# Differential attention pairs: values as the stationary operand in two column tiles, mean square by a product with a block matrix

## The chip, the cores and the metric

The kernel runs on one core of a Trainium2 chip. The metric is the device time of one execution in microseconds. The program is one launch; the host only lays the arrays out.

## The reference, cut to what matters

One layer of a decoder trunk over 256 positions of 1024 features: a SwiGLU mixer, a token mixer of three attention branches, and a second SwiGLU mixer, each followed by a layer norm. The token mixer projects x to queries, keys and values of the three branches and to gates, and merges the branches' outputs by sigmoid gates. Six heads of 64 per branch. The change touches the differential branch alone:

```python
def diff_attention(q, k, v, slopes, lam, subln_g, lambda_init):
    ...
        s = jnp.einsum('bhmcd,bhmsd->bhmcs', qc, k).astype(F32) * scale
        s = jnp.where(dist >= 0, s - slope * dist, -jnp.inf)
        p = jax.nn.softmax(s, axis=-1)
        w = p[:, :, 0] - lam * p[:, :, 1]
        return jnp.einsum('bhcs,bhsd->bhcd', w.astype(v.dtype), v)
    ...
    o = o * lax.rsqrt(jnp.mean(jnp.square(o), axis=-1, keepdims=True) + SUBLN_EPS) * subln_g
    return (o * (1.0 - lambda_init)).astype(v.dtype)
```

So each head has two softmax maps, their weighted difference multiplies the values, and each position's 64 outputs are divided by their root mean square.

## The kernel before

All large products run on TensorE in float32r, with each operand split into a rounded part and a rest: `Weights.split` (L104 to L111) makes both parts of a weight chunk of 128 x 1024, ScalarE the rounded one and VectorE the rest, from a raw buffer that a DMA filled. Nine split buffers and five raw ones go round; `done` gives a buffer back when its products are through, and `pump` splits and loads the next.

The token mixer works through the table `MIX`: projections of queries and keys for one pair of heads (`project`), gate products (`gates`) and branch outputs (`branch`). A pair of heads is a list of stages, and `slot` runs one stage of each pair under way, in the order of the kinds in `KINDS`; so a slot holds, say, the last stage of one pair, the transposes of the next and the scores of a third. The class `Pe` counts TensorE's time as the program is written and starts a slot, at least `PACE` = 10 us after the one before, in the middle of a projection or of gate products. That count only sets the order in which the instructions are written: each engine then works through its own queue in that order and waits for semaphores. For the last 2.2 us before a slot (`QUIET`) no weight split is written.

PSUM has eight banks, four named `acc` and four named `att`. The `att` banks go round: the fifth request takes the first bank again, and the first product in it waits until the bank's last reader is through.

A differential pair has two heads with two maps each, so four score banks (two of each name) and four weight tiles `e` of 128 x 384 (the lower triangle of 256 x 256 in two pieces). Its stages before: `start` makes the scores, the exponentials with their row sums `sm`, and `combine`s e0 + c e1 on VectorE, with c = -lambda sum0/sum1; `turn` transposes the two combined tiles on TensorE and ScalarE copies them to SBUF as `eT`; `pv` multiplies with the transposed weights as the stationary operand (six products with 64 columns), scales the rows by 1/sum0, and computes the mean square on VectorE with the power -1/2 on GpSimd; `scale`, due 2.5 us later, multiplies by it; `turn_o` transposes the output (two transposes), and `act_split` copies it to `oT` and its rest. The other two kinds of pair, `moba_pair` and `stick_pair`, already use `values_T`: the values are the stationary operand, 64 columns for each head of the pair in two column tiles, so that the output comes out transposed.

Of the kernel before, what the change touches and what calls it, by code (L numbers as in the profile page):

```python
# [53 lines left out]
T_M = 3.4  # L54
N_T = 4.5
M_N = 2.0
D_S = 2.5
E_BUFS = 6


class Weights:
# [129 lines left out]
def trunk(ctx: ExitStack, tc: tile.TileContext, start_d, x_d, ln_g, ln_b, gu_d, gun_d, down_d, v_d, qk_d, gate_d,  # L191
# [364 lines left out]
    with ExitStack() as es:  # L556
# [76 lines left out]
        def values_T(b, p, eTs):  # L633

            po = att.tile([P, 512], F32, name="att")
            for kt, cs, ws in ((0, slice(0, S), slice(0, S)), (1, slice(P, S), slice(S, BW))):
                for r in range(2):
                    pe.mm(po[r * HD:(r + 1) * HD, cs], V[:, kt, vcol(b, 2 * p + r)], eTs[r][:, ws], kt == 0, kt == 1,
                          tile_position=(0, r * 64), share=2, skip_group_check=True)
            act_split(oT[b][:, p, 0:S], oT[b][:, p, S:2 * S], po[:, 0:S])  # L640
            pairs_done[b] += 1

# [3 lines left out]

        KINDS = ("sums", "turn_o", "pv", "turn", "valT", "scores")

        def moba_pair(p, qT, kT):
            sm = small.tile([P, 2, 2], F32, name="sm")
# [23 lines left out]
        def diff_pair(p, qT, kT):  # L676
# [4 lines left out]
            def start():  # L681
                banks = [(acc if i < 2 else att).tile([P, 512], F32, name="acc" if i < 2 else "att")
                         for i in range(4)]
                scores([(i * 32, 32, banks[i]) for i in range(4)], qT, kT, True)
                ee.extend(ep.tile([P, BW], F32, name="e") for _ in range(4))
                exp_rows([(banks[i], SLOPES[2 * (2 * p + i // 2) + 1], ee[i], nmx[:, i % 2, i // 2, :],
                           sm[:, i % 2, i // 2, :]) for i in range(4)])
                exps[0] -= 1

                def combine(r):  # L690
                    c = small.tile([P, 2], F32, name="c")
                    nc.vector.reciprocal(c, sm[:, 1, r, :])
                    nc.vector.scalar_tensor_tensor(c, sm[:, 0, r, :], nlam, c, op0=ALU.mult, op1=ALU.mult)
                    e0, e1 = ee[2 * r], ee[2 * r + 1]
                    for t, cs in enumerate((slice(0, P), slice(P, BW))):
                        nc.vector.scalar_tensor_tensor(e0[:, cs], e1[:, cs], c[:, t:t + 1], e0[:, cs],
                                                       op0=ALU.mult, op1=ALU.add)
                for r in range(2):
                    combine(r)

            def pv():
                ps = att.tile([P, 512], F32, name="att")
                for r in range(2):
                    vc, eT = vcol(1, 2 * p + r), eTs[r]
                    o0, o1 = ps[:, r * HD:(r + 1) * HD], ps[:, P + r * HD:P + (r + 1) * HD]
                    pe.mm(o0, eT[:, 0:P], V[:, 0, vc], True, True)
                    pe.mm(o1, eT[:, P:S], V[:, 0, vc], True, False)
                    pe.mm(o1, eT[:, S:BW], V[:, 1, vc], False, True)
                rs = small.tile([P, 2, 2], F32, name="rsm")
                nc.vector.reciprocal(rs, sm[:, 0])  # L710
                o = ep.tile([P, S], F32, name="o", bufs=1)
                o4 = o.rearrange("p (t r c) -> p t r c", t=2, r=2)
                nc.vector.tensor_tensor(
                    o4, ps[:, 0:S].rearrange("p (t r c) -> p t r c", t=2, r=2),
                    rs.rearrange("p r t -> p t r").unsqueeze(3).to_broadcast([P, 2, 2, HD]), op=ALU.mult)
                sq = ep.tile([P, S], F32, name="s1", bufs=3)
                nc.vector.tensor_tensor(sq, o, o, op=ALU.mult)
                ms = small.tile([P, 4], F32, name="ms")
                nc.vector.tensor_reduce(ms, sq.rearrange("p (a c) -> p a c", c=HD), axis=mybir.AxisListType.X,
                                        op=ALU.add)  # L720
                nc.vector.tensor_scalar(ms, ms, 1.0 / HD, EPS, op0=ALU.mult, op1=ALU.add)
                nc.gpsimd.tensor_tensor(ms, ms, mhalf[:, 0:4], op=ALU.pow)
                os_.append(o)

                def scale():
                    nc.vector.tensor_tensor(
                        o4, o4, ms.rearrange("p (t r) -> p t r", t=2).unsqueeze(3).to_broadcast([P, 2, 2, HD]),
                        op=ALU.mult)
                pe.later(D_S, scale)

            def turn_o():
                ps = att.tile([P, 512], F32, name="att")
                for t in range(2):
                    pe.tr(ps[:, t * P:(t + 1) * P], os_[0][:, t * P:(t + 1) * P], ident)
                act_split(oT[1][:, p, 0:S], oT[1][:, p, S:2 * S], ps[:, 0:S])
                pairs_done[1] += 1

            return [{"scores": start},
                    {"turn": lambda: eTs.extend(turn_rows(e) for e in ee[::2])},
                    {"pv": pv},  # L740
                    {"turn_o": turn_o}]

        def stick_pair(p, qT, kT):
            zs, wts, split = [], [], []
# [229 lines left out]
```

## Time and profile before

| what | us |
|---|---|
| median of 3 runs | 598.71 (598.22 to 599.05) |
| the profiled execution | 598.51 |
| its span, first to last instruction | 596.8 |
| TensorE busy | 587.8 (98%) |
| VectorE busy | 407.5 (68%) |
| ScalarE busy | 328.2 (55%) |
| GpSimd busy | 32.4 (5%) |

The profile is of one execution; 1.7 us of its time lie outside the span. PE is TensorE's products, PEld its weight loads (which run beside products), DVE is VectorE, ACT ScalarE, POOL GpSimd, SP the queue that issues the loads. A product's end is modelled, so pieces of the chain, which are cut by start and release, are better prices than its busy time.

### The profile page before, as it was taken

What the parts mean: (1) busy time and instruction counts of PE and PEld (TensorE: products, weight loads), DVE (VectorE), ACT (ScalarE), POOL (GpSimd) and SP (SyncE); (2) the same over time, 40 slices, a digit from 0 to 9 for tenths busy, and PEclk for the clock granted to TensorE, in tenths of its full rate; (3) what the DMA queues carried; (4) which work ended last, traced back from release to release, by engine and by line L of the source; (5) the groups of instructions that cost most, each with busy time, mean ns of one, the idle gap of its engine ahead of it and who ended that gap; (6) DMA issues with size and microseconds to landing.
All of it is one profiled execution on the core that took longest, in us unless ns stands there. A gap on an engine that the chain in (4) does not pass through costs nothing.

```text
span 596.8 us, 8546 instructions
## 1 busy us (share of the span) xinstructions
PE 587.8 (98%) x3150; PEld 505.2 (85%) x3150; DVE 407.5 (68%) x655; ACT 328.2 (55%) x556; POOL 32.4 (5%) x71
## 2 busy tenths in 40 slices
PE   8999999999999999999999999999999999999995
PEld 7888888888888998888888878888898898888884
DVE  6889767674338746597977685889867667774217
ACT  5868656663312758596657654535665655654100
POOL 1610000000001002110001000001000000000001
PEclk9999999999999999999999999999999999999998
DMA  8999755666431576354547447256965565565001
GB/s 320 316 392 314 241 187 180 207 188 226 141 125 63 200 258 237 118 176 150 171 139 245 145 158 264 97 183 217 330 229 177 180 202 186 180 207 178 1 0 70
DMA packets 32538, 113.34 MB, mean 190 GB/s; under 512 B 3681, under 2 KB 4449, under 8 KB 32497
## 3 DMA queue, kind: packets, MB, share of 16 engines
q1 hardware_dynamic: 30672, 106.77, 53.2%
q0 software_dynamic: 1680, 5.83, 3.0%
q8 instruction: 24, 0.39, 0.3%
q10 hardware_dynamic: 144, 0.20, 0.1%
q14 instruction: 18, 0.14, 0.1%
HBM read 111.74 MB, written 1.05 MB: 189 GB/s over the span
## 4 chain that ended last, share of the span: by engine, by line
PE 97%; DMA 1%; DVE 1%; issue 0%; SPq 0%; ACT 0%; DVEq 0%
PE acc L182 91%; PE att L182 4%; PE att L186 2%; DMA sraw<-start 1%; DVE x L364 0%; DVE x L360 0%; ACT w L275 0%; DVE st L448 0%; DVE x L447 0%; SPq L249 0%; DVEq L968 0%; SPq L246 0%; DVE mv L353 0%
## 5 line engine op out<-in xcount | busy, mean ns | idle before, releaser
L107 DVE TENSOR_TENSOR w<-raw,w 128x1024 fp32r<-128x1024 f32 (+1 forms) x166 | 197.8, 1208 | 61.7 <-ACT w L106 60.8
L182 PE MATMUL acc<-xT,w 128*128 128x512 f32 (+1 forms) x1264 | 226.4, 337 | 0.0
L182 PEld LDWEIGHTS acc<-xT,w 128*128 128x128 f32 x1264 | 196.3, 190 | 26.6 <-issue 1.0
L106 ACT ACTIVATE w<-raw 128x1024 fp32r<-128x1024 f32 (+1 forms) x166 | 170.3, 1042 | 52.2 <-PE acc L182 44.0
L182 PE MATMUL acc<-w,xT 128*128 128x512 f32 (+1 forms) x576 | 128.1, 379 | 0.0
L182 PEld LDWEIGHTS acc<-w,xT 128*128 128x128 f32 x576 | 105.5, 188 | 18.6 <-issue 1.0
L182 PE MATMUL acc<-w,hT 128*128 128x512 f32 (+1 forms) x408 | 93.1, 383 | 0.0
L182 PEld LDWEIGHTS acc<-w,hT 128*128 128x128 f32 x408 | 75.2, 188 | 14.9
L475 ACT ACTIVATE lo<-acc 128x256 f32<-128x256 f32 x76 | 28.8, 384 | 57.3 <-PE acc L182 57.3
L477 DVE TENSOR_TENSOR gu<-acc,lo 128x256 f32<-128x256 f32 x76 | 31.6, 423 | 34.7 <-ACT lo L475 34.6
L182 PE MATMUL acc<-xT,wx 128*128 128x256 f32 (+1 forms) x240 | 46.1, 337 | 0.0
L107 DVE TENSOR_TENSOR wx<-raw,wx 128x1024 fp32r<-128x1024 f32 (+1 forms) x30 | 36.3, 1214 | 12.5 <-ACT wx L106 12.5
L182 PEld LDWEIGHTS acc<-xT,wx 128*128 128x128 f32 x240 | 37.5, 190 | 4.4
L106 ACT ACTIVATE wx<-raw 128x1024 fp32r<-128x1024 f32 (+1 forms) x30 | 31.3, 1047 | 11.3 <-PE acc L182 10.2
L354 ACT ACTIVATE rs<-mv 128x1 f32<-128x1 f32 x6 | 1.2, 204 | 59.6 <-DVE mv L353 59.6
L182 PE MATMUL acc<-wx,hT 128*128 128x512 f32 (+1 forms) x138 | 32.8, 380 | 0.0
L182 PEld LDWEIGHTS acc<-wx,hT 128*128 128x128 f32 x138 | 25.2, 188 | 4.9
L355 POOL TENSOR_TENSOR rs<-rs,mhalf 128x1 f32<-128x1 f32 x6 | 5.3, 892 | 407.9 <-ACT rs L354 407.9
L346 DVE SCALAR_TENSOR_TENSOR x<-x,acc 128x512 f32<-128x512 f32 x11 | 7.5, 683 | 27.4 <-PE acc L182 27.4
L182 PE MATMUL acc<-w,oT 128*128 128x512 f32 x108 | 25.7, 393 | 0.0
L182 PEld LDWEIGHTS acc<-w,oT 128*128 128x128 f32 x108 | 20.1, 188 | 4.4 <-issue 0.3
L236 ACT ACTIVATE hT<-gu 128x256 fp32r<-128x256 f32 x38 | 15.8, 417 | 11.5 <-DVE gu L482 11.5
(146 smaller groups left out, 412.9 us busy)
## 6 DMA issues: line engine op xcount, KB each, us to landing
raw<-gu SPq DMA_DIRECT2D x76, 512.0 KB, 4.8
raw<-down SPq DMA_DIRECT2D x44, 512.0 KB, 4.2
raw<-gates SPq DMA_DIRECT2D x24, 512.0 KB, 4.4
raw<-qk SPq DMA_DIRECT2D x18, 512.0 KB, 4.5
raw<-v SPq DMA_DIRECT2D x12, 384.0 KB, 3.0
raw<-w_out SPq DMA_DIRECT2D x8, 512.0 KB, 4.3
raw<-gun SPq DMA_DIRECT2D x8, 512.0 KB, 4.3
sraw<-start SPq DMA_DIRECT2D x7, 384.0 KB, 6.6
```

What stands on the lines that cost most here:

```text
L106: self.nc.scalar.activation(h[:, :n], raw[:, :n], AF.Copy)
L107: self.nc.vector.tensor_tensor(l[:, :n], raw[:, :n], hv[:, :n], op=ALU.subtract)
L182: self.nc.tensor.matmul(out, lhsT=lhsT, rhs=rhs, start=start, stop=stop, **kw)
L186: self.nc.tensor.transpose(out, in_, ident)
L236: nc.scalar.activation(dst_h, src, AF.Copy)
L346: nc.vector.scalar_tensor_tensor(xs, xs, ALPHA, ps[:, 0:n], op0=ALU.mult, op1=ALU.add)
L354: nc.scalar.activation(rs, mv[:, 1:2], AF.Copy, bias=EPS)
L355: nc.gpsimd.tensor_tensor(rs, rs, mhalf[:, 0:1], op=ALU.pow)
L475: nc.scalar.activation(lo, ps[:, S:2 * S], AF.Copy)
L477: nc.vector.tensor_tensor(v, ps[:, 0:S], lo, op=ALU.add)
```

## The change

Of the differential pair, from the exponentials on, everything but the transposes of the weights is rewritten. The rows are now normalised before the values: ScalarE scales the tiles of the first map by 1/sum0, VectorE adds the second map times -lambda/sum1. The values use `values_T`. The output is then transposed already, 64 features of each head on 64 partitions; its square is split into two float32r parts and multiplied by a 128 x 128 block matrix with entries 1/64, which gives each position's mean square on all 64 partitions. The power -1/2 is the exponential of -0.5 times the logarithm on ScalarE, followed by one Newton step on VectorE. `KINDS` and the number of `e` buffers change with it.

```diff
-D_S = 2.5
-E_BUFS = 6
+E_BUFS = 4
...
+            if b == 1:
+                return po
...
-        KINDS = ("sums", "turn_o", "pv", "turn", "valT", "scores")
+        KINDS = ("sums", "turn", "valT", "scores")
...
+        mean64 = ep.tile([P, P], F32R, name="mean64", bufs=1)
...
-                def combine(r):
-                    c = small.tile([P, 2], F32, name="c")
-                    nc.vector.reciprocal(c, sm[:, 1, r, :])
-                    nc.vector.scalar_tensor_tensor(c, sm[:, 0, r, :], nlam, c, op0=ALU.mult, op1=ALU.mult)
+                rs = small.tile([P, 2, 2, 2], F32, name="rsd")
+                nc.vector.reciprocal(rs, sm)
+                nc.vector.tensor_scalar(rs[:, 1], rs[:, 1], nlam, None, op0=ALU.mult)
+                for r in range(2):
                     e0, e1 = ee[2 * r], ee[2 * r + 1]
                     for t, cs in enumerate((slice(0, P), slice(P, BW))):
-                        nc.vector.scalar_tensor_tensor(e0[:, cs], e1[:, cs], c[:, t:t + 1], e0[:, cs],
+                        nc.scalar.activation(e0[:, cs], e0[:, cs], AF.Copy, scale=rs[:, 0, r, t:t + 1])
+                    for t, cs in enumerate((slice(0, P), slice(P, BW))):
+                        nc.vector.scalar_tensor_tensor(e0[:, cs], e1[:, cs], rs[:, 1, r, t:t + 1], e0[:, cs],
                                                        op0=ALU.mult, op1=ALU.add)
...
-            def pv():
+            def values():
+                po = values_T(1, p, eTs)
+                o = ep.tile([P, S], F32, name="o", bufs=1)
+                nc.scalar.activation(o, po[:, 0:S], AF.Copy)
+                sq = ep.tile([P, S], F32, name="s1", bufs=3)
+                nc.vector.tensor_tensor(sq, po[:, 0:S], o, op=ALU.mult)
+                sp = ep.tile([P, 2 * S], F32R, name="sq", bufs=1)
+                act_split(sp[:, 0:S], sp[:, S:2 * S], sq)
+                os_.extend((o, sp))
+
+            def rms():
+                o, sp = os_
                 ps = att.tile([P, 512], F32, name="att")
...
-            def turn_o():
-                ps = att.tile([P, 512], F32, name="att")
-                for t in range(2):
-                    pe.tr(ps[:, t * P:(t + 1) * P], os_[0][:, t * P:(t + 1) * P], ident)
-                act_split(oT[1][:, p, 0:S], oT[1][:, p, S:2 * S], ps[:, 0:S])
+                for n in range(2):
+                    pe.mm(ps[:, 0:S], mean64, sp[:, n * S:(n + 1) * S], n == 0, n == 1)
+                f = ep.tile([P, S], F32, name="s1", bufs=3)
+                nc.scalar.activation(f, ps[:, 0:S], AF.Ln, bias=eps_c)
+                nc.scalar.activation(f, f, AF.Exp, scale=-0.5)
+
+                c = ep.tile([P, S], F32, name="s1", bufs=3)
+                nc.vector.scalar_tensor_tensor(c, ps[:, 0:S], EPS, f, op0=ALU.add, op1=ALU.mult)
+                nc.vector.tensor_tensor(c, c, f, op=ALU.mult)
+                nc.vector.tensor_scalar(c, c, -0.5, 1.5, op0=ALU.mult, op1=ALU.add)
+                nc.vector.tensor_tensor(o, o, f, op=ALU.mult)
+                nc.vector.tensor_tensor(o, o, c, op=ALU.mult)
+                act_split(oT[1][:, p, 0:S], oT[1][:, p, S:2 * S], o)
                 pairs_done[1] += 1
...
                     {"turn": lambda: eTs.extend(turn_rows(e) for e in ee[::2])},
-                    {"pv": pv},
-                    {"turn_o": turn_o}]
+                    {"valT": values},
+                    {"sums": rms}]
```

The order on TensorE in the slot that holds the last stage of the first differential pair, before. The `att` numbers tell the requests apart; `e` are the tiles of the third differential pair, which are transposed, and `kT`, `qT` make the first MoBA pair's scores.

```order
L186 MATMUL att_3034<-ident_117,o_2864 128x128 x2
L182 MATMUL att_3039<-V_1892,eT_2876 128x64 x3
L182 MATMUL att_3039<-V_1892,eT_2882 128x64 x3
L186 MATMUL att_3056<-ident_117,e_2896 128x128 x3
L186 MATMUL att_3062<-ident_117,e_2898 128x128 x3
L182 MATMUL att_3068<-kT_3017,qT_3013 128x128
L182 MATMUL att_3069<-kT_3017,qT_3013 128x128
```

The same slot on TensorE after the change.

```order
L181 MATMUL att_3039<-sq_2886,mean64_2136 128x256 x2
L185 MATMUL att_3053<-ident_117,e_2901 128x128 x3
L185 MATMUL att_3059<-ident_117,e_2903 128x128 x3
L181 MATMUL att_3065<-eT_2869,V_1892 64x256
L181 MATMUL att_3065<-eT_2875,V_1892 64x256
L181 MATMUL att_3065<-eT_2869,V_1892 64x128
L181 MATMUL att_3065<-eT_2875,V_1892 64x128
L181 MATMUL att_3077<-kT_3022,qT_3018 128x128
L181 MATMUL att_3078<-kT_3022,qT_3018 128x128
```

Six banks are requested in the slot both times, from four; the two score banks are the slot's first and second request come round again. Before, these were the banks of the output's transposes and of the values; now they are those of the mean square (att_3039) and of the first transposed weights (att_3053).

ScalarE's queue from the projection's copies (`s1`) to the next weight split (`w`) in that slot, before.

```order
L826 ACTIVATE s1_3012<-acc_2978,qsc_215 128x256
L829 ACTIVATE s1_3016<-acc_2979 128x256
L236 ACTIVATE oT1_1894<-att_3034 128x256
L630 ACTIVATE eT_3060<-att_3056 128x384
L630 ACTIVATE eT_3066<-att_3062 128x384
L106 ACTIVATE w_3080<-raw_2829 128x1024
```

The same piece of ScalarE's queue after the change; L729 is the logarithm, L730 the exponential, L716 the values' copy.

```order
L829 ACTIVATE s1_3017<-acc_2983,qsc_215 128x256
L832 ACTIVATE s1_3021<-acc_2984 128x256
L729 ACTIVATE s1_3042<-att_3039,eps_c_2142 128x256
L730 ACTIVATE s1_3042<-s1_3042 128x256
L235 ACTIVATE oT1_1894<-o_2882 128x256
L629 ACTIVATE eT_3057<-att_3053 128x384
L629 ACTIVATE eT_3063<-att_3059 128x384
L716 ACTIVATE o_3070<-att_3065 128x256
L235 ACTIVATE sq_3074<-s1_3072 128x256
L105 ACTIVATE w_3089<-raw_2839 128x1024
```

The copy to `oT1` read the transposes' bank before; now it reads `o_2882`, the result of VectorE's last product, and stands ahead of the copies of the transposed weights `eT`.

VectorE's queue in that slot after the change, from the projection's end to the first score reduction.

```order
L833 TENSOR_TENSOR kT_3022<-acc_2984,s1_3021 128x256
L733 SCALAR_TENSOR_TENSOR s1_3045<-att_3039,s1_3042 128x256
L734 TENSOR_TENSOR s1_3045<-s1_3045,s1_3042 128x256
L735 TENSOR_SCALAR s1_3045<-s1_3045 128x256
L736 TENSOR_TENSOR o_2882<-o_2882,s1_3042 128x256
L737 TENSOR_TENSOR o_2882<-o_2882,s1_3045 128x256
L236 TENSOR_TENSOR oT1_1894<-o_2882,oT1_1894 128x256
L718 TENSOR_TENSOR s1_3072<-att_3065,o_3070 128x256
L236 TENSOR_TENSOR sq_3074<-s1_3072,sq_3074 128x256
L615 ISA e_3083,nmx_3038<-att_3077,base_195 128x128
```

Only the first of these five operations of the mean square (L733 to L737) reads a PSUM bank; the copy to `oT1` on ScalarE needs the fifth.

## Rows read from the trace of the kernel before

**Rows 1.** The page: busy time by engine, and the chain that ended last.

```profile
PE 587.8 (98%) x3150; PEld 505.2 (85%) x3150; DVE 407.5 (68%) x655; ACT 328.2 (55%) x556; POOL 32.4 (5%) x71
PE 97%; DMA 1%; DVE 1%; issue 0%; SPq 0%; ACT 0%; DVEq 0%
```

**Rows 2.** The chain in order of time: start us, length us, engine, tile, line, count.

```profile
285.71 1.28 PE att L182 x12
...
302.07 0.22 PE att L186 x2
302.29 1.29 PE att L182 x12
303.57 0.66 PE att L186 x6
...
313.06 0.22 PE att L186 x2
...
324.12 0.87 PE att L186 x8
...
349.91 0.80 PE att L182 x8
```

**Rows 3.** Timeline of one slot: start us, length us, what; in brackets the wait before it.

```profile
301.38 0.42 DVE L830 TENSOR_TENSOR kT<-acc,s 128x256 f32<-128x256 f32 x1 [0.38 <-ACT s L829]
301.80 0.25 PEld L186 LDWEIGHTS att<-ident,o 128*128 128x128 f32 x2
...
302.32 0.38 ACT L236 ACTIVATE oT<-att 128x256 fp32r<-128x256 f32 x1 [0.98 <-PE att L186]
302.74 0.42 DVE L237 TENSOR_TENSOR oT<-att,oT 128x256 fp32r<-128x256 f32 x1 [0.94 <-ACT oT L236]
...
303.94 0.87 ACT L630 ACTIVATE eT<-att 128x384 f32<-128x384 f32 x2 [1.24 <-PE att L186]
...
304.16 0.52 PEld L182 LDWEIGHTS att<-kT,qT 64*128 64x128 f32 x8 [0.17 <-DVE o L713]
...
305.12 0.29 DVE L616 CUSTOM_DVE_ANT_0 e<-att,base 128x128 f32<-128x128 f32 x1
```

**Rows 4.** Groups by line and shape: count, busy us, mean ns, idle before.

```profile
L182 PE MATMUL acc<-xT,w 128*128 128x256 f32 x632 | 82.2, 284 | 0.0
...
L481 ACT ACTIVATE gu<-gu 128x256 f32<-128x256 f32 x38 | 15.5, 408 | 0.3 <-DVE gu L477 0.3
...
L827 DVE SCALAR_TENSOR_TENSOR qT<-acc,qsc,s 128x256 f32<-128x256 f32 x9 | 4.3, 481 | 5.7 <-ACT s L826 5.7
L826 ACT ACTIVATE s<-acc,qsc 128x256 f32<-128x256 f32 x9 | 4.2, 467 | 10.6 <-PE acc L182 10.6
...
L236 ACT ACTIVATE oT<-att 128x256 fp32r<-128x256 f32 x9 | 3.5, 385 | 10.4 <-PE att L182 6.1 <-PE att L186 4.3
...
L668 DVE TENSOR_SCALAR e<-e,rsm 128x256 f32<-128x256 f32 x6 | 2.1, 349 | 0.0
...
L717 DVE TENSOR_TENSOR s<-o 128x256 f32<-128x256 f32 x3 | 1.3, 425 | 0.1
```

**Rows 5.** Timeline behind the second differential pair's exponentials.

```profile
281.36 0.16 DVE L692 RECIPROCAL c<-smd 128x2 f32<-128x2 f32 x1
...
281.62 0.19 ACT L622 ACTIVATION_READ_ACCUMULATOR e<-e,nmxd 128x1 f32 x1
...
283.98 0.41 DVE L830 TENSOR_TENSOR kT<-acc,s 128x256 f32<-128x256 f32 x1
```

**Rows 6.** Timeline at the start of the slot near 324 us.

```profile
323.62 1.28 DVE L110 SCALAR_TENSOR_TENSOR w<-raw,g,w 128x1024 fp32r<-128x1024 f32 x1
...
323.96 0.38 PE L186 MATMUL att<-ident,o 128*128 128x128 f32 x2
```

**Rows 7.** Span's end (timeline; stretches, with granted clock as PEclk) and start (group).

```profile
588.27 1.24 PE L182 MATMUL acc<-w,hT 128*128 128x256 f32 x9
...
591.40:591.50 0.10, 0.00 (x0) 0.00 (x0) 0.10 (x2) 0.00 (x0) 0.10 (x1) 0.59 0.00 0
...
L256 PE MATMUL att<-warm 128*128 128x128 f32 x14 | 3.4, 432 | 1.1 <-DVE warm L252 1.1
```

More of the change, by code (lines that the diff above doesn't have):

```diff
@@ L644, in trunk @@
         pairs_done = [0, 0, 0]
-        KINDS = ("sums", "turn_o", "pv", "turn", "valT", "scores")
+        KINDS = ("sums", "turn", "valT", "scores")
+        mean64 = ep.tile([P, P], F32R, name="mean64", bufs=1)
+        m32 = ep.tile([P, S], F32, name="s1", bufs=3)
+        nc.gpsimd.memset(m32, 0.0)
+        for r in range(2):
+            nc.gpsimd.memset(m32[r * HD:(r + 1) * HD, r * HD:(r + 1) * HD], 1.0 / HD)
+        nc.gpsimd.tensor_copy(mean64, m32[:, 0:P])
+        eps_c = small.tile([P, 1], F32, name="eps_c", bufs=1)
+        nc.gpsimd.memset(eps_c, EPS)
         def moba_pair(p, qT, kT):
@@ L688, in start @@
                 exps[0] -= 1
-                def combine(r):
-                    c = small.tile([P, 2], F32, name="c")
-                    nc.vector.reciprocal(c, sm[:, 1, r, :])
-                    nc.vector.scalar_tensor_tensor(c, sm[:, 0, r, :], nlam, c, op0=ALU.mult, op1=ALU.mult)
+                rs = small.tile([P, 2, 2, 2], F32, name="rsd")
+                nc.vector.reciprocal(rs, sm)
+                nc.vector.tensor_scalar(rs[:, 1], rs[:, 1], nlam, None, op0=ALU.mult)
+                for r in range(2):
@@ L697, in combine @@
                                                        op0=ALU.mult, op1=ALU.add)
-                for r in range(2):
-                    combine(r)
-            def pv():
-                ps = att.tile([P, 512], F32, name="att")
[L703 to L729, printed above, removed]
```

## The prediction

> **What bounds the kernel now.** Read the page first: TensorE is busy 587.8 of 596.8 us, and the chain that ended last lies 97% on it [rows 1]. So a microsecond that TensorE gains is a microsecond of the kernel, and so is one that it waits; VectorE (68%), ScalarE (55%) and GpSimd (5%) count only where TensorE waits for them. Next comes that chain in order of time, in the stretch where the differential pairs lie. Three slots of the hand-written order carry the change, and I call them R1 (302.07), R2 (313.06) and R3 (324.12): in each the last stage of one differential pair stands first, then the transposes of another pair, and the scores of a third stand last. The chain gives pieces without a hole, so the prices of the stages can be read as differences of start times [rows 2]: the last transposes 0.22, the six value products of a differential pair 1.29, six transposes 0.66, and the column-tiled values of the other two kinds of pair 0.80. Last, the timeline of R1 shows what the other engines do there: ScalarE and VectorE have finished the next projection at 301.80, ScalarE begins the copy of the transposed output at 302.32, copies the transposed weights at 303.94, and the weight load of the scores stands 0.17 us behind VectorE's reading of a PSUM bank [rows 3]. That small wait is the thing to keep in mind: the slot takes six banks from a pool of four, so the first score bank is the one that the slot's first stage took, and the second is the one of its second stage.
>
> **The change, part by part.**
>
> TensorE. In the slot at 285.71 and in R1 and R2 the six value products (1.29) become four column-tiled ones (0.80, the same shape as the row at 349.91) [rows 2]: 3 x 0.49 = 1.5 us gained. In R1 to R3 two transposes (0.22) become two products of 256 columns; 632 of those took 82.2 us of busy time, 0.13 each [rows 4], so 0.22 to 0.26: nothing, or 0.1 us lost in all. The Trainium skill, TensorEngine Tiling (Array Packing), section Theoretical Speedup, promises up to 2x for two column tiles. By it a pair's values would fall from 1.29 to about 0.65 and the gain would be 1.9 instead of 1.5; the row at 0.80 decides, since it holds the change of tiling as well.
>
> ScalarE before a slot. Each pair gets four scaling copies behind its eight exponentials. Nearest row: the copy with a scale per partition, 0.47 for 256 columns [rows 4]; four cost at most 1.9, and since half of them are narrower I take 1.5. They stand in the queue ahead of the next projection's copies. In the slot of the second pair the exponentials ended at 281.81 and the projection was through at 284.39 [rows 5]. Before the scaling come two small VectorE operations, 0.16 for the nearest of that size [rows 5], and three handovers of 0.04 (a copy ended at 302.70, VectorE started on it at 302.74 [rows 3]); so the projection is 2.0 to 2.4 later, 286.4 to 286.8. The scores that want it come at 285.7 + 0.66 + 0.80 = 287.2. Hidden, with 0.4 to 0.8 to spare; if that cover were gone, what lies beyond it would be lost once in each of two slots, and I keep 0.5 for it in the range. The weight splits behind them, and the loads that wait for a raw buffer to come free from a split, are late by as much; they serve products of the next slot.
>
> The removed VectorE work (reductions, GpSimd's power, the second scaling) was beside TensorE's products; its removal pays nothing. The four buffers in place of six are free of charge too: a slot's transposes, which release the weights, stand ahead of the scores that take the buffers. The setup of the block matrix is on GpSimd, 5% busy [rows 1].
>
> The new wait. In R1 to R3 the mean square now ends in a chain across ScalarE and VectorE, and ScalarE's queue has its last copy **ahead of** the copies of the transposed weights (see the order rows). Those copies release the bank that the second score product needs. I count from the slot's first weight load, t = 0 (301.80 in R1), with prices from [rows 4] and 0.04 per handover:
> ScalarE began 0.52 after that load in R1 [rows 3]; with twice the columns 0.6. Logarithm, priced as the scaled copy from PSUM, 0.47: 1.07. Exponential, as the 0.41 activation from SBUF: 1.52. VectorE's first operation reads PSUM, 0.48: 2.04; this frees the first score bank. Product 0.42: 2.50. Scale and add 0.35: 2.89. Product 0.42 at once behind it: 3.31. Product 0.42: 3.77. ScalarE's copy 0.39 to 0.42: 4.2. First copy of transposed weights, half of the 0.87 for two: 4.6. Now TensorE may go on.
> TensorE itself is ready for the scores at 0.22 + 0.66 + 0.80 = 1.68. It waits 0.35 for the first bank, issues one product, and waits for the second: **2.9 us lost in each of R1, R2 and R3**. Queued behind it are the rest of the scores and the projection's products, the work that bounds the kernel. Behind the waiting copy on ScalarE stand the other copy, the values' two copies and the weight splits; on VectorE, behind the second value copy (ScalarE free at 5.1, copy 0.4, square 0.4, copy 0.4, split 0.4, handovers), the score reductions begin near 6.8 instead of 305.12 - 301.80 = 3.3 [rows 3].
> In R3 something more is late. VectorE's last weight split before it ended at 324.90, 0.94 after that slot's first transposes at 323.96 [rows 6]. Its queue in R2 runs 6.8 - 3.3 = 3.5 later, the next slot only 2.9 - 0.5 = 2.4 later, so that split ends near 0.9 + 1.1 = 2.0 where the chain wants VectorE at 1.56: 0.5 more.
>
> The logarithm is not in the trace with this shape. If it and every VectorE operation cost what the cheapest row of 256 columns does (0.35), a slot loses 2.5; if a 1.28 us weight split stands in front of the chain in each slot, 4.2.
> Sum: 3 x 2.9 + 0.5 - 1.5 = +7.7 us. The profiled execution took 598.51 (span 596.8, and 1.7 around it), so 606.2; the median of the runs, 598.71, lies 0.2 above it: **606.4 us**.
>
> **The rivals.**
>
> The clock falls in the waits. At the end of the span the last product ended at 589.51 and the granted clock went from full (2.4 GHz) to half (1.2 GHz) within 591.40 to 591.50, where it averages 0.59: 1.9 us later, with TensorE idle in between [rows 7]. A wait of 2.9 us, broken by one short product, is longer than that; against it, the run-up to this fall was a stretch that got thinner, and the waits are between dense stretches. Price: at the start the 14 warm-up products took 3.4 us [rows 7], near 0.22 apart, where products of 128 columns stand 0.11 apart later (0.66 for six [rows 2]): about 1.5 us until full speed. One fall makes 607.9, three make 610.9. The Trainium skill, TensorE: Matmul & The Clock Gate, section HAM oscillation, describes this mechanism for waits between bursts; that no row of this kernel shows a fall between bursts is because it has had no such wait.
>
> No wait: faster. This needs the chain to be through before TensorE wants the second bank, that is, t = 4.6 would have to be 1.7; it decides once the loss per slot is under 0.5. Then only the gain is left: 598.7 - 1.5 = 597.2. For it: the slot had six banks before, and waited 0.17. Against it: five dependent VectorE operations alone are 2.1 us.
>
> Only the first bank waits, because the transposed weights' copies come free in another way. Then 0.35 per slot: 3 x 0.35 - 1.5 = -0.4, no change that can be told. Against it: the order of ScalarE's queue.
>
> Late weights. Some 3.4 us more of ScalarE per pair (1.5 scaling, 0.4 + 0.4 values, 0.9 logarithm and exponential) could hold up splits until TensorE waits for them: one chunk late is one split on each engine, 1.0 + 1.2 = 2.2, on top 608.6. Against it: the chunks are split ahead of use by most of a slot.
>
> **How the numbers follow.** The waits without a fall of the clock, 606.4, own range 604.0 to 608.5: 0.55. Waits with one or more falls, 608 to 611: 0.25. Late weights as well: 0.08. Shorter waits for a reason that I don't see, 600 to 604: 0.03. First bank only: 0.04. No wait: 0.05. The range 603.5 to 611.0 leaves out the last three and a little of the first tail. Faster by over 0.2% (1.2 us, about what a measurement of this kernel can tell from no change) 0.06, with a hundredth from the first-bank case; same 0.04 with a little of the shorter waits; slower 0.90.
>
> **What would show it.** TensorE's idle time, near zero before, should have two entries in each of R1 to R3: a short one put down to VectorE's first operation on the mean square, and one of about 2.5 us put down to ScalarE's copy of the transposed weights. The value pieces should read 0.80 where they read 1.29. The slots' distance should grow by 2.4 us, and nothing outside 285 to 330 should change. I am wrong if TensorE's idle time is under 2 us in all, if the wait is named for a weight split, or if the granted clock in 300 to 335 is under full speed: then the rival's price, not mine, makes the time.

## The result: 2.3% slower, and above the range

The changed kernel took 612.03 us (median of 6 runs, 610.02 to 616.07) beside 598.85 us for the kernel before (6 runs, 598.22 to 599.08): ratio 1.0231, 95% interval 1.0209 to 1.0253. The prediction had 606.4 and a range up to 611.0. The profiled execution took 616.07, span 614.4 after 596.8, so 17.6 us have to be found.

Start with TensorE's waits in the changed kernel. Each row names the engine and the line that ended the wait, then the us in total, the number of waits and the longest.

```profile
PE att L181 <- ACT eT L629: 5.8, 3, 1.9
PE att L255 <- DVE warm L251: 1.1, 1, 1.1
```

The second row is the start of the span, as before. The first is new: three waits, all for ScalarE's copies of transposed weights. The timeline of R1 shows the order of events (start, length, engine, line).

```profile
302.70 0.30 PEld L181 LDWEIGHTS att<-sq,mean 128*128 128x128 f32 x2
...
303.25 0.47 ACT L729 ACTIVATE s<-att,eps_c 128x256 f32<-128x256 f32 x1 [1.05 <-PE att L181]
...
303.80 0.87 PE L181 MATMUL att<-eT,V 128*64 128x256 f32 x8
...
304.21 0.42 DVE L733 SCALAR_TENSOR_TENSOR s<-att,s 128x256 f32<-128x256 f32 x1 [1.55 <-ACT s L730]
...
304.69 0.29 PEld L181 LDWEIGHTS att<-kT,qT 64*128 64x128 f32 x2 [0.26 <-DVE s L733]
...
305.12 0.29 DVE L735 TENSOR_SCALAR s<-s 128x256 f32<-128x256 f32 x1
...
306.24 0.42 ACT L235 ACTIVATE oT<-o 128x256 fp32r<-128x256 f32 x1 [2.07 <-DVE o L737]
306.57 0.85 ACT L629 ACTIVATE eT<-att 128x384 f32<-128x384 f32 x2
...
307.09 0.52 PEld L181 LDWEIGHTS att<-kT,qT 64*128 64x128 f32 x6 [2.11 <-ACT eT L629]
```

Where [rows 3] had one wait of 0.17, there are now two: a short one for VectorE's first operation, which frees the first score bank, and the long one. ScalarE stood idle 2.07 us at its oT copy, with the copies that TensorE needed behind it. So far it is as predicted. The chain that ended last, in order of time (start, length, engine, tile, line, count), with the pieces that answer to [rows 2], shows two things that are not.

```profile
21.43 165.93 PE acc L181 x869
...
287.76 0.80 PE att L181 x8
...
302.98 0.25 PE att L181 x2
...
307.09 0.92 PE att L181 x4
308.01 10.14 PE acc L181 x41
318.15 0.25 PE att L181 x2
...
322.33 1.65 PE att L181 x5
323.98 11.08 PE acc L181 x44
335.05 0.26 PE att L181 x2
...
339.23 1.65 PE att L181 x5
340.88 13.46 PE acc L181 x47
...
450.30 156.81 PE acc L181 x831
```

The value piece (287.76) reads 0.80 where it read 1.28, as predicted. But the slots stand 15.2 and 16.9 us apart where R1 to R3 stood 11.0 and 11.1, more than the waits make. And the first and the last row are the two feed-forward stages, which the change does not touch. In the kernel before they read:

```profile
21.81 164.22 PE acc L182 x869
...
434.38 155.15 PE acc L182 x831
```

They grew by 1.71 and 1.66 us. The slots' growth beyond the waits goes with the granted clock (PEclk, the third number from the right; 1.00 is full) in stretches of time:

```profile
300.00:308.00 8.00, 6.07 (x50) 4.99 (x49) 5.21 (x12) 3.19 (x8) 0.00 (x0) 1.00 0.56 182
308.00:312.00 4.00, 4.00 (x15) 3.37 (x15) 3.52 (x12) 3.82 (x10) 0.00 (x0) 0.57 0.00 0
312.00:314.00 2.00, 2.00 (x10) 1.62 (x9) 1.94 (x7) 0.72 (x3) 0.00 (x0) 1.00 0.82 256
...
322.00:328.00 6.00, 5.67 (x22) 4.83 (x23) 3.22 (x13) 4.49 (x15) 0.00 (x0) 0.51 0.02 5
...
340.00:346.00 6.00, 6.00 (x17) 4.28 (x14) 4.16 (x14) 3.70 (x10) 0.00 (x0) 0.50 0.24 89
```

After each wait TensorE worked for a while at about half clock, 1.2 instead of 2.4 GHz. That is the prediction's rival with the clock. What grew in the feed-forward stages is the distance from one product to the next. Here are the same twelve products, before and then after (start, time, count):

```profile
136.00 2.88 PE L182 MATMUL acc<-wx,hT 128*128 128x512 f32 x12
138.72 2.66 PE L182 MATMUL acc<-w,hT 128*128 128x512 f32 x11
```

```profile
135.87 2.96 PE L181 MATMUL acc<-wx,hT 128*128 128x512 f32 x12
138.67 2.49 PE L181 MATMUL acc<-w,hT 128*128 128x512 f32 x10
```

From the first to the thirteenth product it is 2.72 us before and 2.80 after: 226.7 and 233.3 ns each. Products with xT stationary have kept their distance, some 227 ns. All products with hT or oT stationary and 512 moving columns have the new one: the 1.7 us in each feed-forward stage and an estimated 0.7 for the 108 products with oT are 4.1 us. What the change does to them is to move their tiles. The pool `small` (each of the four tiles named here takes up 32 bytes per partition and has four buffers, but for the last) lost `c` and `ms` and gained `rsd` and a single `eps_c`: 128 + 128 - 128 - 32 = 96 bytes less. hT, V and oT, which lie behind this pool, begin 96 bytes earlier. (Where tiles begin is reckoned here and below from the sizes in the program; the traces hold no addresses.)

So the theory has four terms: the gain of 1.5, the waits, 4.1 for the tiles' start, and the clock. The last three each have a rival: that the waits come from the amount of new work and not from its place in the queues, that the starts are innocent, and that the half clock is not the waits' doing.

### The profile page after: what moved, and what is told of

It is laid out like the page before. It is cut to its first block, busy times and chain, and to the rows that moved or that the text cites. A ratio compares the mean times of both kernels' runs of the same rounds, so it can differ in the third digit from the quotient of the medians.

```text
span 614.4 us, 8548 instructions
## 1 busy us (share of the span) xinstructions
PE 600.0 (98%) x3138; PEld 509.6 (83%) x3138; DVE 409.7 (67%) x652; ACT 336.9 (55%) x580; POOL 30.1 (5%) x73
## 4 chain that ended last, share of the span: by engine, by line
PE 95%; DVE 1%; ACT 1%; DMA 1%; issue 0%; SPq 0%; DVEq 0%; ACTq 0%
PE acc L181 90%; PE att L181 4%; PE att L185 1%; DMA sraw<-start 1%; ACT s L729 0%; DVE o L737 0%; DVE s L734 0%; DVE s L733 0%; ACT s L730 0%; ACT oT L235 0%; ACT eT L629 0%; DVE x L363 0%; DVE o L736 0%; DVE s L735 0%; SPq L248 0%
## 5 line engine op out<-in xcount | busy, mean ns | idle before, releaser
L181 PE MATMUL acc<-xT,w 128*128 128x512 f32 (+1 forms) x1264 | 229.3, 340 | 0.0
L181 PEld LDWEIGHTS acc<-xT,w 128*128 128x128 f32 x1264 | 198.9, 192 | 27.4 <-issue 1.3
L181 PE MATMUL acc<-w,xT 128*128 128x512 f32 (+1 forms) x576 | 131.9, 386 | 0.0
L181 PEld LDWEIGHTS acc<-w,xT 128*128 128x128 f32 x576 | 108.0, 192 | 20.0 <-issue 1.5
L181 PE MATMUL acc<-w,hT 128*128 128x512 f32 (+1 forms) x408 | 95.6, 389 | 0.0
L181 PEld LDWEIGHTS acc<-w,hT 128*128 128x128 f32 x408 | 75.2, 188 | 17.5
```

Source lines behind the costliest of these rows:

```text
L181: self.nc.tensor.matmul(out, lhsT=lhsT, rhs=rhs, start=start, stop=stop, **kw)
```

## The experiments

Medians, with the ratio to the kernel before on the same chip and its 95% interval. "Start as before" is the changed kernel with `eps_c` given four buffers in place of one, which puts the 96 bytes back.

**Where tiles begin.** First the kernel before, with 32 unused bytes ahead of hT:

```diff
+    pad = small.tile([P, 1], F32, name="pad", bufs=1)
+    nc.gpsimd.memset(pad, 0.0)
```

> The kernel before, with one unused tile of 32 bytes per partition ahead of the mixers' tiles, so that hT, V, oT, qT and e begin 32 bytes past a multiple of 64, as in the changed kernel; nothing else is moved. Theory (the start of the stationary operand sets the products' distance): the 512-wide products with hT or oT stationary stand 233.3 ns apart instead of 226.7, the FFN's two pieces of the chain grow to about 165.9 and 156.8 us, and the run takes 598.85 + 4.1 = 602.9 us. Rival (the 6.7 ns came with the changed stretch, through other queues or a clock a little under full): distances stay 226.7, 598.9 us.

602.75 us, ratio 1.0065 (1.0053 to 1.0077): the theory, to 0.2 us, with one unused tile and nothing of the change. The pieces of its chain:

```profile
21.82 165.91 PE acc L182 x869
...
436.72 156.76 PE acc L182 x831
```

Then the other way, the changed kernel with 32 bytes more (`eps_c` with bufs=2):

> The changed kernel, with a second buffer of eps_c: 32 bytes more, by which hT and what lies behind it begin at a multiple of 64 again. Theory: distances back to 226.7 ns, 4.1 us less than the changed kernel in the same state of the clock; with waits of 2.5 us in R1 to R3 left, 598.85 - 1.5 + 7.5 = 604.9 us when no wait brings the clock down, and up to 8.5 more, 613.4, when all three do as in the profiled execution. Rival (the start is not the cause): distances stay 233.3, 609.0 to 617.5.

606.76 us (605.68 to 607.52), 1.0133 (1.0116 to 1.0149). Better than the changed kernel, but the feed-forward pieces are 164.78 and 155.62, and the products 228.9 ns apart. That is a third level: of the 4.1 us the two stages alone still hold 1.0. "A multiple of 64" is not the rule. Two more steps of the pad (bufs=2 and bufs=3) in the kernel before:

> The kernel before with 64 unused bytes, so that hT, V, oT, qT and e begin at a multiple of 128, where in the kernel before they begin 64 bytes past one. In the changed kernel with 32 bytes more they begin at a multiple of 128 too, and there the FFN's two pieces of the chain stayed 0.56 and 0.47 us longer than before. Theory (the start decides, in three steps so far: 64 past a multiple of 128 gives 226.7 ns, 0 past gives 228.9, 96 past gives 233.3): pieces of 164.8 and 155.6, and 480 products 2.2 ns later each, with those on oT 1.3 us in all: 599.9 us. Rival (what was left there came from the changed stretch, not from the start): pieces as before, 598.6.

602.43 us, 1.0062 (1.0050 to 1.0075), 233.3 ns. The theory of that moment, "past a multiple of 128", fell: the second kernel also began at such a multiple and had 228.9.

> The kernel before with 96 unused bytes: starts 32 past a multiple of 128. Theory (what counts is the distance from a multiple of 64): as 96 past, 233.3 ns and 602.8 us. Rival (four different steps, or only 96 past is bad): another distance, between 226.7 and 233.3, and 598.6 to 602.8.

603.40 us, 1.0075 (1.0062 to 1.0087), 234.3 ns; neither theory's number exactly. What was left open was whether hT's own start counts or its start against the moving weights, which had not moved in any of these. So all tiles together, the pad at the front of the first pool:

```diff
+    pad = const.tile([P, 8], F32, name="pad")
+    nc.gpsimd.memset(pad, 0.0)
     g8 = const.tile([P, 1], F32, name="g8")
```

> The kernel before with one unused tile of 32 bytes at the very front, so that every tile on the chip, the moving weights and xT too, begins 32 bytes later, and none stands otherwise to another than in the kernel before. So far hT began 0, 32, 64, 96, 160 and 192 past the starts of the moving weights in steps of 256, with distances of 226.7, 233.3, 233.3, 234.2, 233.3 and 228.9 ns. Theory A (what counts is where a product's stationary operand begins against its moving one): all distances stay as before, 598.8 us. Theory B (what counts is the stationary operand's own start): all 512-wide products grow as those on hT did, some 1,750 by about 6.7 ns, 610 us or more; at the least those on hT and oT, 602.9.

598.59 us, 0.9992 (0.9983 to 1.0001), and the twelve products take 2.72 us again:

```profile
136.44 2.88 PE L182 MATMUL acc<-wx,hT 128*128 128x512 f32 x12
139.16 2.20 PE L182 MATMUL acc<-w,hT 128*128 128x512 f32 x9
```

Here hT begins where it did in the first experiment, to the byte, and costs nothing; the difference is that the tiles ahead of it went along. So what counts is where hT begins against something ahead of it. That this is the moving weights is argued: of the tiles ahead, they are what these products read. The table has all that was measured. The start is that of hT past the moving weights' start, counted within 256 bytes; 160 and 192 are 96 and 64 bytes earlier than in the kernel before, and whether the pattern repeats every 256 bytes was not tried. The ns are the mean distance of all back-to-back products with hT stationary in the two stages.

| start | kernels | ns per product | the two stages, us |
|---|---|---|---|
| 0 | before; all 32 later; start as before | 226.7 | 164.22, 155.15 |
| 32 | before + 32 | 233.3 | 165.91, 156.76 |
| 64 | before + 64 | 233.3 | 165.92, 156.73 |
| 96 | before + 96 | 234.3 | 166.16, 157.00 |
| 160 | the changed kernel | 233.3 | 165.93, 156.81 |
| 192 | changed + 32 | 228.9 | 164.78, 155.62 |

**The change without the starts.**

> The changed kernel with the start of hT as in the kernel before (96 bytes more), nothing else. Theory: gain and waits alone, 598.9 - 1.5 + 7.5 = 604.9 us in executions whose clock stays full, 1.7 more for each short fall; distances 226.7. Rival (something of the change costs time outside its stretch and the starts): above 605.5 with full clock and with the FFN's pieces as before.

606.40 us (605.12 to 612.91), 1.0148 (1.0115 to 1.0180). The stages are back at 164.22 and 155.15. The fastest execution, 605.12, is gain and waits alone to 0.2 us, as expected; the profiled one (606.36) has one stretch at half clock:

```profile
306.00:310.00 4.00, 4.00 (x17) 3.19 (x18) 3.06 (x12) 3.51 (x9) 0.00 (x0) 0.57 0.00 0
...
318.00:326.00 8.00, 6.00 (x40) 4.75 (x37) 4.81 (x18) 4.74 (x17) 0.00 (x0) 1.00 0.26 73
...
332.00:340.00 8.00, 6.00 (x33) 4.46 (x30) 5.82 (x17) 5.13 (x15) 0.00 (x0) 1.00 0.36 134
```

Its three waits are of one length (1.9 each), yet the clock fell behind R1's and not behind the other two.

**The clock.** Sixteen products that no output uses fill the wait, first in the kernel with 32 bytes more:

```diff
+            if (b, p) in ((1, 1), (1, 2), (0, 0)):
+                for _ in range(16):
+                    nc.tensor.matmul(po[:, S:2 * S], lhsT=mean64, rhs=xT[:, 0, 0:S], start=True, stop=True)
             if b == 1:
                 return po
```

> The changed kernel with the 32 bytes more, and 16 products of 256 columns behind the value products of R1 to R3, written to an unused half of their bank: TensorE works some 1.9 us in what was its wait. They add work that no output uses. Theory (the idle time brings the clock down): the slots stay as long as in the kernel with the 32 bytes alone, the granted clock stays full in 300 to 350, and every execution is near 604.9, at most 606, with a narrow interval. Rival (the clock falls for another reason, not for TensorE's idle time): half clock in 300 to 350 as before, 608 to 613, with the same spread of the single times.

606.27 us (606.0 to 606.52), 1.0126 (1.0112 to 1.0139). This decides nothing: the profile of that kernel without the products was at full clock too, and the time is 1.4 above what was expected, 1.0 of it what is left of the starts' cost in the two stages. The same products in the changed kernel itself:

> The changed kernel, start of hT left as it is (233.3 ns), with the 16 products of 256 columns behind the value products of R1 to R3, which no output uses. Theory (TensorE's idle time in the waits brings the clock down, and that is the spread of the changed kernel's times): full clock in 300 to 350, every execution at 598.9 - 1.5 + 7.5 + 4.1 = 609.0 or up to 0.7 above, none over 610.5, where the changed kernel has 610.0 to 616.1. Rival (the half clock has another cause, or the spread has): half clock again, 610 to 616.

609.05 us, and nothing above 609.33; 1.0169 (1.0156 to 1.0182). The slot R1 is as long as with the wait (5.03 from its first product to the projection's, both times). TensorE is busy through, and the clock is full:

```profile
303.64 0.24 PE att L181 x2
303.87 0.66 PE att L185 x6
304.53 0.80 PE att L181 x8
305.33 2.10 PE att L641 x16
307.43 1.24 PE att L181 x6
308.67 8.54 PE acc L181 x41
```

The piece behind the slot takes 8.54 where it took 10.14. More work made the kernel 3.0 us faster at the median (four executions): that is the half clock's share of the changed kernel's median, and nearly all of its spread.

**The wait.** The Newton step left out (start as before), which takes four of VectorE's five operations off the chain:

```diff
-                nc.vector.scalar_tensor_tensor(c, ps[:, 0:S], EPS, f, op0=ALU.add, op1=ALU.mult)
-                nc.vector.tensor_tensor(c, c, f, op=ALU.mult)
-                nc.vector.tensor_scalar(c, c, -0.5, 1.5, op0=ALU.mult, op1=ALU.add)
                 nc.vector.tensor_tensor(o, o, f, op=ALU.mult)
-                nc.vector.tensor_tensor(o, o, c, op=ALU.mult)
```

> The changed kernel with the start of hT as in the kernel before (96 bytes more), and without the Newton step behind the logarithm and exponential, which leaves that correction of the root out: four of VectorE's five operations of the chain go. Theory (the chain's length is the wait): VectorE's part falls from 2.1 to 0.45 us, so each wait for the transposed weights shrinks from 2.1 to about 0.5 and the loss per slot from 2.5 to 0.9; the clock stays full: 598.6 - 1.5 + 3 x 0.9 = 599.8 us. Rival (the wait is set by ScalarE's own queue, not by VectorE's part): 2 us remain in each slot, 603.5 or more.

600.30 us, 1.0024 (1.0015 to 1.0033); three waits of 0.5 are left of those of 1.9. The chain's length sets the wait's length. Next, its last copy on VectorE, so that ScalarE no longer stands still with the transposed weights behind:

```diff
-                act_split(oT[1][:, p, 0:S], oT[1][:, p, S:2 * S], o)
+                nc.vector.tensor_copy(oT[1][:, p, 0:S], o)
+                nc.vector.tensor_tensor(oT[1][:, p, S:2 * S], o, oT[1][:, p, 0:S].bitcast(F32), op=ALU.subtract)
```

> The changed kernel with the start of hT as in the kernel before, and the rounding copy to oT at the chain's end on VectorE instead of ScalarE; the order of the stages is that of the change. Theory (ScalarE stands still in its queue at that copy, and the copies of the transposed weights behind it are what TensorE waits for): ScalarE is through with the exponential at 1.5 us of the slot and with the transposed weights at 2.4, VectorE frees the first bank at 2.0; TensorE waits 0.4 in each slot instead of 2.5: 598.7 - 1.5 + 1.2 = 598.4 us, no difference from before. Rival (VectorE's part of the chain holds up something else, reductions, a normalisation or a split): TensorE waits there, 1 to 4 us more, 599.5 to 602.5.

599.88 us, 1.0022 (1.0012 to 1.0032). The three long waits for eT are gone, with one copy moved: the queue's order made them. In their place stands one wait in R3, for the second pair's normalisation, which VectorE reaches late; so the rival is right too. Three of the eleven executions took 601.45 to 601.75, with a mean granted clock of 0.993 to 0.995 where the others have 0.996 or more; none of the three was profiled.

```profile
PE att L185 <- DVE e L679: 1.6, 1, 1.6
```

**Is there a place for the chain?** Four orders of the same work. The transposes first (with 32 bytes more):

```diff
-        KINDS = ("sums", "turn", "valT", "scores")
+        KINDS = ("turn", "sums", "valT", "scores")
```

> The previous kernel with the transposes of the next pair ahead of the mean square's products in R1 to R3, so that ScalarE copies the transposed weights ahead of the logarithm. Theory (the second score bank waits for the copies that stand behind the chain): TensorE's two entries of idle time in R1 to R3 go, the granted clock stays full in 300 to 350, and only the gain of the value products is left: 598.85 - 1.5 = 597.3 us. Rival 1 (the chain then holds up what stands behind it, value copies and weight splits, and TensorE waits for these): part of the 7.5 us comes back under another name, 599 to 603. Rival 2 (the scores wait for ScalarE's longer work at large): the wait stays, 604.9 or more.

604.38 us, 1.0094 (1.0080 to 1.0109). R1 and R2 run without a wait, R3 has one of 2.7:

```profile
PE att L185 <- DVE e L679: 2.7, 1, 2.7
```

VectorE's timeline shows what stands ahead of that normalisation: the chain, the squares at its end, and two weight splits.

```profile
320.92 0.42 DVE L236 TENSOR_TENSOR sq<-s,sq 128x256 fp32r<-128x256 f32 x1 [0.48 <-ACT sq L235]
...
325.16 2.48 DVE L109 SCALAR_TENSOR_TENSOR w<-raw,g,w 128x1024 fp32r<-128x1024 f32 x2 [0.49 <-ACT w L108]
327.56 0.17 DVE L676 RECIPROCAL rsm<-sm 128x4 f32<-128x4 f32 x1
327.76 1.01 DVE L679 TENSOR_SCALAR e<-e,rsm 128x128 f32<-128x128 f32 x4
```

Behind this one wait the clock fell too (0.82 in 326 to 330, 0.75 in 330 to 334). With the start as before and the normalisation ahead of the two splits:

```diff
-M_N = 2.0
+M_N = 1.0
```

> The whole change with the start of hT as in the kernel before, the transposes ahead of the mean square's products, and the second pair's normalisation handed to VectorE 1 us after the scores instead of 2, by which it stands ahead of two weight splits (2.5 us) in R2. Nothing is left out. Theory (the 2.7 us wait in R3 was these two splits ahead of the normalisation, with VectorE late by the chain): the normalisation runs as soon as its exponentials are done, TensorE waits 0.6 at most, clock full: 597.2 to 597.9 us, faster than before. Rival (VectorE's load is the matter, and the splits, now later, are waited for in their turn): 1.5 to 3 us of wait under another name, 599 to 601.

600.45 us, 1.0026 (1.0017 to 1.0036). The wait for the normalisation is gone, and others stand in the rows: a gate's bank that VectorE empties late, and one copy of transposed weights.

```profile
PE acc L181 <- DVE G L871: 1.3, 1, 1.3
...
PE att L181 <- ACT eT L629: 0.5, 1, 0.5
```

The mean square 4 us behind the pair's own values:

```diff
                 os_.extend((o, sp))
+                pe.later(4.0, rms)
...
-                    {"valT": values},
-                    {"sums": rms}]
+                    {"valT": values}]
```

> The changed kernel with the start of hT as in the kernel before, and the mean square's products 4 us behind the pair's own value products, in the middle of the next projection, instead of at the head of the next slot. Nothing is left out. Theory (the wait comes from the chain's place ahead of the copies of the transposed weights, and behind the score reductions there is room): no wait in R1 to R3, full clock, 598.6 - 1.5 = 597.1 us, faster than before. Rival (ScalarE and VectorE have no room for some 3.5 us more per pair wherever it stands, as where the transposes went ahead): TensorE waits for a normalisation or a weight split, 2 to 6 us, 599 to 603.

601.64 us, 1.0054 (1.0041 to 1.0066): 1.5 for the gate's bank near 301, 1.7 for eT in R3, where the chain again stood ahead on ScalarE. Square and chain spread over the slot, transposes first, last copy on VectorE as above (the two functions hold the lines of the change, `o` has two buffers):

```diff
+                pe.later(2.8, square)
...
+                pe.later(4.4, chain)
```

> The whole change with the start of hT as in the kernel before, the transposes first, and the work of the mean square spread in the slot: square and split behind the second pair's normalisation, the chain with its Newton step behind these, its last copy on VectorE. Nothing is left out. Theory (TensorE's waits come from what stands ahead of transposed weights and normalisations in two queues, not from the amount of work): no wait, 597.2 us, faster than before. Rival (VectorE has no room for the chain in any place): it is late for the reductions of the next scores, and TensorE waits for a normalisation or a split, 2 to 4 us, 599 to 602.

600.46 us, 1.0029 (1.0019 to 1.0040). TensorE is busy through 300 to 330, and waits 2.3 for the gate's bank behind that, near 336; there VectorE has one pair's chain ahead of the gate's operation. And the transposes first without the Newton step:

> The changed kernel with the start of hT as in the kernel before, the transposes ahead of the mean square's products, and the Newton step left out. With the transposes ahead and the Newton step kept, VectorE ran 3.1 us late into R3, where TensorE waited for a normalisation. Theory (VectorE's load after the chain made that wait; without four operations, 1.6 us a pair, it has room): no wait in R1 to R3, full clock, 598.7 - 1.5 = 597.2 us, faster than before. Rival (the wait came from the order, with ScalarE at the chain's last copy, not from VectorE's load): 1 to 3 us of wait remain, 598.2 to 600.5.

598.34 us, 0.9989 (0.9980 to 0.9997): 0.8 is still waited for one normalisation. It is the only version of the changed kernel that is not slower than the kernel before. What it gains is about 0.1%, under the 0.2% that the prediction set as what can be told from no change, and it leaves the correction out.

## Why the prediction was wrong

The sum in its own terms, each with what showed it:

| term | predicted | measured |
|---|---|---|
| value products | -1.5 | -1.5: 0.80 where [rows 2] has 1.28, in three slots |
| waits in R1 to R3 | 3 x 2.9 + 0.5 = +9.2 | 2.50 + 2.57 + 2.56 = +7.6 |
| outside the slots | 0 | +4.1 |
| clock, in no term | 0, a rival at 0.25 | +1.0 to +7 in single executions, +3.0 at the median |

The waits come from the chain: R1 without the projection's products took 3.02 before (302.07 to 305.09) and 5.03 after (302.98 to 308.01) with 0.49 less work; R2 and R3 are taken at full clock, from the kernel with 32 bytes more (5.10 and 5.09, beside 3.02 and 2.53 before, where R3 has no gain). 598.85 - 1.5 + 7.6 + 4.1 = 609.05, which the filled kernel has, and 3.0 more make 612.05. The profiled execution had more of the clock: against the filled kernel its slots are 1.6 (R1), 3.0 and 3.1 longer, 7.7 in all. So -1.5 + 7.6 + 4.1 + 7.7 = 17.9, and since its first feed-forward stage began 0.4 earlier (21.43 after 21.81), 17.5 of the 17.6 us are found.

The step that failed is the sentence "nothing outside 285 to 330 should change". The prediction priced the operations that came and went, but the tiles that came and went it put at nothing: of the buffers it asked only which stage releases them, and not what lies behind them. The runs showed 4.1 us there. Neither this nor the clock alone leaves the range: 609.05 lies in it, and so does the median of the kernel with the start as before. The two together carry the time out.

The waits were right in place, order and releaser, and too long by 0.4 a slot. From the slot's first weight load (302.70) TensorE went on at 4.39 where 4.6 was predicted; among the shorter steps are VectorE's first operation (0.42, not 0.48) and its third (0.29, not 0.35). And TensorE was ready for the scores later than counted, at 1.97 and not at 1.68, when its value products were through (304.67): the 1.68 is a sum of pieces that begin with the slot's first product, and this stands 0.28 behind the load (302.98). The 0.5 for a late split in R3 did not come: there the chain began on VectorE 1.30 after the slot's first product, in R1 1.23.

That the kernel with the start as before has a median of 606.40, the predicted number, is luck: its waits are 1.6 shorter than predicted, and the clock, which is in no term, gives about as much back.

The likeliest case was the wrong one of the two with waits. The prediction saw that a wait of this length is longer than the 1.9 us after which the clock had fallen at the span's end [rows 7], and gave it 0.25 since the wait stands between dense stretches. That was no protection: in the profiled execution the clock fell at all three. Nor was the stretch ahead of the fall at the span's end thinner, as the prediction has it: TensorE was busy 2.00 of the 2.00 us from 587 to 589, and its last product ended at 589.51. The price of 1.5 fits one fall only: R1's piece went from 8.5 to 10.1, while R2 and R3 grew by 3.0 and 3.1. The Trainium skill, TensorE: Matmul & The Clock Gate, section HAM oscillation, describes waits between bursts behind which each next burst starts at the lower clock. The changed kernel's trace agrees, with 0.50 to 0.57 granted behind its three waits; the kernel with the start as before does not, with one fall behind three such waits, nor does that with 32 bytes more, with none in its profiled execution.

What held: the scaling copies were hidden (the slot with the values at 287.76 runs without a gap), late weights did not appear (the parts of that rival's 3.4 us more of ScalarE per pair add up to 3.2), and TensorE's idle entries have the predicted names. The "no wait" rival fails at its condition: each order that took the chain from in front of TensorE but kept its operations met another wait, in each of them at least one for something that VectorE did late. VectorE (the third engine in the row) had little room in this stretch even in the kernel before: it was busy 23.95 of 30 us, where the prediction went by the 68% of the whole span [rows 1]:

```profile
300.00:330.00 30.00, 30.00 (x192) 25.22 (x191) 23.95 (x69) 20.36 (x49) 3.10 (x4) 1.00 0.54 177
```

What decides whether the clock falls at a given wait stays open. The kernel with the start as before shows one fall at three equal waits, and times from 605.1 to 612.9.

## What to carry to other kernels

When a change adds or drops any tile, compare where the tiles behind it begin, against the operand that they are multiplied with; 96 bytes cost more here than the optimisation could gain. Where an engine's queue holds a copy that waits on another engine's chain, look at what is queued behind that copy before counting operations. A wait on TensorE costs itself and, at times, as much again in clock; a cheap test is to fill it with products that nobody reads.

## What the runs showed of the hardware

Products of 512 moving columns with hT stationary stood 226.7, 228.9, 233.3 or 234.3 ns apart, by where hT begins against the tiles ahead of it, the moving weights among them (six starts, table above); moving all tiles together changed nothing. Why is not shown. TensorE's granted clock fell to half at waits of 1.9 to 2.7 us in some profiled executions (all three of the changed kernel, one of three with the start as before, the one of 2.7 with the transposes first). In others it stayed full behind waits of the same length (1.9 with 32 bytes more, 2.3 with the work spread).
